# Output projection and feed-forward layer in four blocks of 512 prompt tokens and two passes over the weights, with the sample's tokens computed apart

## The chip, the cores and the metric

The kernel runs on one core of a Trainium2 chip. The core has five engines with instruction streams of their own: TensorE (PE, matmuls; its weight loads are listed as PEld), VectorE (DVE), ScalarE (ACT), GpSimd (POOL) and SyncE (SP). In this kernel nearly all transfers between DRAM and the on-chip memory SBUF are issued by SP, one behind the other: a transfer that has to wait for something holds up every transfer behind it on SP. Matmuls write into PSUM, which has eight banks of 128 x 512 fp32 numbers.

The metric is the device time of one execution in microseconds (us), the median of several runs.

## The reference

One layer with two groups of tokens: a prompt of 2048 tokens, and a sample of 8 streams with 16 tokens each (128 tokens), which have modulation vectors of their own for each stream. Model width is 1024 (8 chunks of 128), feed-forward width 2816 (22 chunks of 128). The change concerns the last lines of the layer:

```
mix = jnp.concatenate([conv_out, attn], axis=-1) @ w_out
x = x + g1 * mix
h = _rmsnorm(x, norm2_g) * (1 + sc2) + sh2
x = x + g2 * ((jax.nn.silu(h @ w_gate) * (h @ w_up)) @ w_down)
```

What lies ahead of these lines (input projection, convolution, attention) is the same code in both kernels.

## The kernel before

All numbers are fp32. For TensorE each operand is split into two fp32r parts, high and low (`parts_of`: ScalarE copies the high part, VectorE subtracts for the low one), and each product is three matmuls: high x high, low x high, high x low. Activations are transposed: 128 channels on the partitions, tokens along the columns.

**Token blocks.** The 2176 tokens (prompt and sample together) form six blocks, `HALVES`, of 368, 368 and four times 360 columns; the sample is the end of the last block. Two blocks form a pair; `PAIRS` has three.

**Output projection** (`project_out`, L1169). For each block eight accumulators take all eight PSUM banks, one for each chunk of output channels. For each of eight input chunks c, in `OUT_ORDER`, a tile of the concatenated input is loaded from DRAM (`cr<-cat_d`, a ring of four), passed through Swish for c < 4, split into `ch` and `cl`, and multiplied: 8 x 3 matmuls. Then for each of the eight banks the input x is loaded (`xo<-xT`, a ring of 20 tiles), `scaled_add` (L1141) puts x + g1 * mix into it, it is written to DRAM (`x_d<-xo`), ScalarE squares it and POOL adds the squares up (`ssum`, L1210). `root` (L1223 on) makes the reciprocal square root of the mean, with small matmuls on TensorE. The x tiles of blocks 0 and 1 stay in SBUF; pair 0 is normed from them behind block 2 (`norm`: POOL's product at L1253, ScalarE's scale and shift, VectorE's subtractions in `right_sides`).

**Feed-forward layer** (`ffn_up`, `ffn_down`). A pair's two blocks, and the two halves of the weights, make 2 x 2 block products, computed with seven products (q = 0 to 6) of sums instead of eight. `right_sides` writes the seven right sides to DRAM (`ht_d` for the up products, `gt_d` for the down products), `sums` writes the sums of weights (`sup_d`, `sdn_d`). For each pair, up has 11 column blocks f (each of two chunks u), 14 products of 12 matmuls in each; down has seven q with four products of 33 matmuls. With three pairs that is 5544 + 2772 = 8316 matmuls (L1440). Products take turns in the eight banks. The norms of pairs 1 and 2 are woven into the up products of pair 0.

**What sets the order.** Each engine's stream is in the order in which the program and its scheduler emit it. `pump` loads ahead: whenever a product has been emitted, it fills the free slots of the rings W (left sides, 6, later 10) and T (right sides, 8, later 29). Right sides pass through raw tiles of their own (`traw`, 6); weights through quarters (`rR`, 12, later 15). The pump starts only at the end of block 4 of the projection.

Of the kernel before, what the change touches and what calls it, by code (L numbers as in the profile page):

```python
# [1 line left out]

# [4 lines left out]
F32 = mybir.dt.float32  # L7
# [32 lines left out]
HALVES = [(0, 368), (368, 736), (736, 1096), (1096, 1456), (1456, 1816), (1816, 2176)]  # L40
NW = 368
PAIRS = [(HALVES[i][0], HALVES[i][1] - HALVES[i][0]) for i in (0, 2, 4)]
# [14 lines left out]
BANK8 = ("u", "cv", "tr", "u", "ss", "u", "cv", "tr")  # L57
# [61 lines left out]
class Layer:  # L119
# [30 lines left out]
    def run(self, stop=99):  # L150
# [3 lines left out]
        with ExitStack() as ctx:  # L154
# [12 lines left out]
            self.ht_d = d.tile([P, 3, 7, 4, NW], F32, name="ht_d")  # L167
            self.r_d = d.tile([len(HALVES), P, NW], F32, name="r_d")
            self.gt_d = d.tile([P, 3, 7, NF // 2, NW], F32, name="gt_d")
# [940 lines left out]
    def out_projection(self, stop):  # L1110
        self.L.close()
        with ExitStack() as c0:
            self.rings(c0)
            with ExitStack() as c1:
                self.project_out(c1)
            self.LB.close()
            self.grow(c0)
            with ExitStack() as c1:
                self.ffn_up(c1)
            with ExitStack() as c1:  # L1120
                self.ffn_down(c1)

# [4 lines left out]
    def accumulate(self, acc, terms, n, first, last):  # L1127

        for j, z in enumerate(acc):
            m = slice(j * P, (j + 1) * P)  # L1130
            for i, (hi, lo, yh, yl) in enumerate(terms):
                for k, (w, y) in enumerate(((hi, yh), (lo, yh), (hi, yl))):
                    self.nc.tensor.matmul(z[:, :n], w[:, m], y, start=(first and i == 0 and k == 0),  # L1133
                                          stop=(last and i == len(terms) - 1 and k == 2))

    def scaled_add(self, z, v, j, x, b0, b1):

        nc = self.nc
        n, npr = b1 - b0, min(b1, T) - b0
        m = self.mod[v][:, j, :]  # L1140
        nc.vector.scalar_tensor_tensor(x[:, :npr], z[:, :npr], m[:, 0:1], x[:, :npr], ALU.mult, ALU.add)  # L1141
        if npr < n:
            zv, xv = sample_view(z[:, npr:n]), sample_view(x[:, npr:n])
            nc.vector.tensor_tensor(zv, zv, per_stream(m[:, 1:9]), ALU.mult)
            nc.vector.tensor_tensor(xv, xv, zv, ALU.add)
# [6 lines left out]
    def split_rows(self, hi, lo, src, ring, tag):  # L1152

        for i in range(2):
            t = slice(512 * i, 512 * i + 512)
            raw = ring.tile([P, 512], F32, tag=tag, name="raw")
            self.queued(self.nc.sync.dma_start(raw, src[:, t]))
# [497 lines left out]
```

## Time and profile before

| | us |
|---|---|
| median of 3 runs | 2840.87 (2839.73 to 2841.87) |
| the profiled execution, its own time | 2842.93 |
| its span in the profile | 2841.2 |

The profile is of one execution. A page of it gives each engine's busy time and share of the span; other views give the chain of work that ended last (each step followed back to what released it), busy time by stretch of the span, groups of instructions by line and shape, single instructions in order of time with the idle time ahead of them, and what SP waited for. A row such as `L1440 PE MATMUL z<-rT,rW` names the line, the engine, the operation and the tiles written and read. A busy matmul row's mean is the time from its start to its end; since matmuls overlap in the pipeline, the spacing between them is shorter, and is read from starts or from a stretch in which TensorE never stops. The granted clock of TensorE is given as a share of full speed. The lines that matter stand where they are used, below.

### The profile page before, as it was taken

What the parts mean: (1) busy time and instruction counts of PE and PEld (TensorE: products, weight loads), DVE (VectorE), ACT (ScalarE), POOL (GpSimd) and SP (SyncE); (2) the same over time, 40 slices, a digit from 0 to 9 for tenths busy, and PEclk for the clock granted to TensorE, in tenths of its full rate; (3) what the DMA queues carried; (4) which work ended last, traced back from release to release, by engine and by line L of the source; (5) the groups of instructions that cost most, each with busy time, mean ns of one, the idle gap of its engine ahead of it and who ended that gap; (6) DMA issues with size and microseconds to landing.
All of it is one profiled execution on the core that took longest, in us unless ns stands there. A gap on an engine that the chain in (4) does not pass through costs nothing.

```text
span 2841.2 us, 48479 instructions
## 1 busy us (share of the span) xinstructions
PE 2729.4 (96%) x16536; PEld 2521.3 (89%) x16536; DVE 2160.8 (76%) x4235; ACT 1435.3 (51%) x2812; POOL 506.0 (18%) x685
## 2 busy tenths in 40 slices
PE   7899999989988999999998999999999999999999
PEld 6899988866666777788998999999999999999999
DVE  3698898988786788635488899777797778676765
ACT  4443323357675777754354455444454446555552
POOL 3454411243232222213202020000000000000000
PEclk9999999988899999999998999999999999999999
DMA  8763567674236656355667678776786669788883
GB/s 306 247 196 113 176 220 255 189 204 124 82 110 175 191 182 185 116 174 189 212 238 232 237 264 287 255 229 208 227 296 213 217 209 310 245 281 257 271 255 117
DMA packets 390024, 603.23 MB, mean 212 GB/s; under 512 B 46240, under 2 KB 249152, under 8 KB 387728
## 3 DMA queue, kind: packets, MB, share of 16 engines
q1 hardware_dynamic: 375312, 574.72, 62.6%
q0 software_dynamic: 14464, 25.42, 3.7%
q8 instruction: 130, 2.13, 0.3%
q14 instruction: 118, 0.97, 0.1%
HBM read 421.97 MB, written 178.07 MB: 211 GB/s over the span
## 4 chain that ended last, share of the span: by engine, by line
PE 78%; DMA 9%; DVE 6%; ACT 3%; issue 3%; POOL 2%; SPq 1%; DVEq 0%; ACTq 0%; POOLq 0%
PE z L1440 44%; PE z L510 7%; PE pv L957 5%; PE acc L1133 4%; PE pa L320 3%; PE pvv L340 3%; PE pg L320 3%; PE s L966 2%; PE s L967 2%; PE mx L927 2%; DMA vraw<-o_v 1%; DVE M L930 1%; DMA wraw<-w_in 1%; DMA k_d<-qp 1%; PE lane L1096 1%
## 5 line engine op out<-in xcount | busy, mean ns | idle before, releaser
L1440 PE MATMUL z<-rT,rW 128*128 128x360 f32 (+1 forms) x8316 | 1382.6, 328 | 5.1 <-ACT oR L1240 1.9
L1440 PEld LDWEIGHTS z<-rT,rW 128*128 128x128 f32 x8316 | 1379.4, 188 | 6.9 <-ACT oR L1240 2.3
L1149 ACT ACTIVATE rW<-rR 128x512 fp32r<-128x512 f32 x714 | 435.1, 617 | 397.9 <-PE z L1440 285.6
L1150 DVE TENSOR_TENSOR rW<-rR,rW 128x512 fp32r<-128x512 f32 x714 | 477.6, 673 | 154.7 <-ACT rW L1149 150.8
L698 DVE SCALAR_TENSOR_TENSOR cv<-cu,cpar,cv 128x384 f32<-128x384 f32 x580 | 311.6, 616 | 2.6 <-ACT cv L696 2.5
L957 PE MATMUL pv<-e,V 128*128 128x512 f32 (+3 forms) x960 | 265.0, 381 | 22.6 <-ACT e L1149 13.1
L957 PEld LDWEIGHTS pv<-e,V 128*128 128x128 f32 x960 | 168.9, 192 | 68.3 <-ACT e L1149 15.2
L930 DVE TENSOR_REDUCE M<-mx 128x1 f32<-128x512 f32 (+2 forms) x320 | 190.1, 605 | 50.5 <-PE mx L927 34.9
L971 ACT ACTIVATE ef<-s 128x512 f32<-128x512 f32 (+3 forms) x320 | 166.0, 529 | 104.8 <-PE s L967 46.7
L510 PE MATMUL z<-hqx,wqh 128*128 128x384 f32 (+1 forms) x768 | 196.6, 333 | 1.3 <-DVE logf L347 1.3
L1149 ACT ACTIVATE rT<-traw 128x360 fp32r<-128x360 f32 (+1 forms) x315 | 149.9, 501 | 88.8 <-DMA traw<-gt_d 52.5
L1150 POOL TENSOR_TENSOR e<-ef,e 128x512 fp32r<-128x512 f32 (+3 forms) x106 | 127.0, 1198 | 364.4 <-ACT e L1149 182.1
L1150 DVE TENSOR_TENSOR rT<-traw,rT 128x360 fp32r<-128x360 f32 (+1 forms) x315 | 158.4, 533 | 41.3 <-ACT rT L1149 41.0
L1150 DVE TENSOR_TENSOR e<-ef,e 128x512 fp32r<-128x512 f32 (+3 forms) x214 | 147.3, 698 | 40.8 <-ACT e L1149 38.1
L1149 ACT ACTIVATE e<-ef 128x512 fp32r<-128x512 f32 (+3 forms) x320 | 174.2, 565 | 4.4
L510 PEld LDWEIGHTS z<-hqx,wqh 128*128 128x128 f32 x768 | 135.7, 188 | 19.2 <-issue 15.5
L927 PE MATMUL mx<-K,Q 96*128 96x512 f32 (+2 forms) x320 | 133.6, 426 | 15.3 <-DVE M L930 13.2
L1133 PE MATMUL acc<-ch,woh 128*128 128x360 f32 (+1 forms) x384 | 128.4, 336 | 9.9 <-ACT ch L1149 5.0
L1368 DVE TENSOR_TENSOR rR<-rR 128x512 f32<-128x512 f32 (+1 forms) x136 | 90.5, 683 | 54.6 <-DMA rR<-w_down 50.0
L966 PE MATMUL s<-Q,K 128*128 128x512 f32 (+3 forms) x320 | 126.7, 397 | 3.2 <-ACT ef L971 3.0
L1133 PE MATMUL acc<-ch,wol 128*128 128x360 f32 (+1 forms) x384 | 128.1, 334 | 0.0
L510 PE MATMUL z<-hqx,wql 128*128 128x384 f32 (+1 forms) x384 | 126.4, 329 | 0.0
(306 smaller groups left out, 3955.5 us busy)
## 6 DMA issues: line engine op xcount, KB each, us to landing
rR<-sup_d SPq DMA_DIRECT2D x176, 256.0 KB
rR<-w_gate SPq DMA_DIRECT2D x132, 256.0 KB
traw<-gt_d SPq DMA_DIRECT2D x154, 180.0 KB
rR<-w_down SPq DMA_DIRECT2D x104, 256.0 KB
rR<-sdn_d SPq DMA_DIRECT2D x96, 256.0 KB
rR<-w_up SPq DMA_DIRECT2D x88, 256.0 KB
sup_d<-rR SPq DMA_DIRECT2D x88, 256.0 KB
wa<-w_ada SPq DMA_DIRECT2D x16, 1024.0 KB
```

The source lines that it names most:

```text
L320: nc.tensor.matmul(pz[:, :n], w[:, m], x[:, :n], start=(c == 0 and k == 0), stop=(c == CB - 1 and k == 2))
L510: nc.tensor.matmul(z[:, :n], w[:, m], x[:, :n], start=(c == 0 and k == 0), stop=(c == CB - 1 and k == 2))
L698: self.pin(nc.vector.scalar_tensor_tensor(dst, src, w, acc[i], ALU.mult, ALU.add))
L927: nc.tensor.matmul(mx[:, :w], Q2[0:AUX, h, j * P:(j + 1) * P], K2[kb][0:AUX, h, :w], start=True, stop=not diag)
L930: nc.vector.tensor_reduce(M[:, i, kb:kb + 1], mx[:, :w], AX.X, ALU.max)
L957: nc.tensor.matmul(z[h][:, off:], V[kt // 4][:, v, kt % 4, h:h + 2, :].rearrange("p b c -> p (b c)"), e[:, x, off:], start=(kt == 0 and i ...
L966: nc.tensor.matmul(s[:, off:], K1[kb][:, h, sl], Q1[:, h, off:], start=True, stop=False)
L971: nc.scalar.activation(ef[:, off:], s[:, off:], AF.Exp)
L1133: self.nc.tensor.matmul(z[:, :n], w[:, m], y, start=(first and i == 0 and k == 0), stop=(last and i == len(terms) - 1 and k == 2))
L1149: self.nc.scalar.activation(hi, raw, AF.Copy)
L1150: engine.tensor_tensor(lo, raw, f32(hi), ALU.subtract)
L1440: nc.tensor.matmul(z, W[:, x, m], t[:, y, :w], start=(k == 0 and i == 0), stop=(k == n - 1 and i == 2))
```

## The change

The blocks are now four of 512 prompt columns, the widest that a bank holds, in two pairs, so that the weights are gone through twice. The 128 sample tokens leave the blocks. Their activations become left sides (`lhsT`) of plain products with 512 columns of weights, in three places: between blocks 1 and 2 of the projection (`sample`, 48 matmuls), in the up products of pair 1 (`sample_up`, 264 matmuls, weights `w_gu` loaded and split for it) and in the down products of pair 0 from its product 6 on (`sample_down`, 132 matmuls, weights `w_dn`, left sides `gS` loaded from `gs_d`). Their results come out transposed and are turned back by 8 + 22 + 8 transposes on TensorE.

Counts: products of the feed-forward layer 4 x 1386 = 5544 matmuls in place of 8316, and 396 for the sample; projection 768 + 48 in place of 1152. All have 512 columns.

To make room in SBUF the buffers change:

| | before | after |
|---|---|---|
| x tiles of the projection | 20 | 5 |
| raw tiles | cat 4, w_out 3, right sides 6, weights in their quarters | one ring of 5 for cat and w_out and first right sides; 4 in up pass 0; then one ring of 5 for left and right sides, sample's weights and `gS` |
| T slots | 8, later 29 | 8, 24 with block 3 of the projection (in the room of w_out), 28 |
| W slots | 6, later 10 | 6, 7 from up pass 1 |
| banks that products rotate in | 8 | 5 (the sample uses the others) |
| x of pair 0 for its norm | kept in SBUF | loaded again (`nx<-x_d`) |

Pair 0's norm is spread over block 2 (two steps behind each c), drained behind it, and the pump starts there, ahead of block 3 in the program. The core of the diff:

```diff
-HALVES = [(0, 368), (368, 736), (736, 1096), (1096, 1456), (1456, 1816), (1816, 2176)]
-PAIRS = [(HALVES[i][0], HALVES[i][1] - HALVES[i][0]) for i in (0, 2, 4)]
-BANK8 = ("u", "cv", "tr", "u", "ss", "u", "cv", "tr")
+NW = 512
+HALVES = [(b, b + NW) for b in range(0, T, NW)]
+PAIRS = [(HALVES[i], HALVES[i + 1]) for i in (0, 2)]
+BANK5 = ("u", "cv", "u", "cv", "u")
+SAMPLE_AT = (0, 2, 4, 5, 7, 9, 11, 12)
...
+    def loaded(self, t, src, func=None, queued=False):
+        pool, tag, n = self.raw
+        raw = pool.tile([P, 512], F32, tag=tag, name="raw", bufs=n)[:, :src.shape[-1]]
+        load = self.nc.sync.dma_start(raw, src)
...
+        self.parts_of(hi, lo, raw, self.nc.vector)
...
     def project_out(self, ctx):
+        self.raw = cp, "cr", 5
...
+        def block(b0, b1, work):
+            acc = self.accumulators()
+            tail = []
+            for i, c in enumerate(OUT_ORDER):
+                tail.append((*weights(c), cat(c, b0, b1)))
+                if b1 < T or i < CB - 2:
+                    self.accumulate(acc, tail, i == 0, i == CB - 1)
+                    tail = []
+                for _ in range(2):
+                    next(work, None)
...
-                x = sp.tile([P, NW], F32, tag="x", name="xo", bufs=20)
+                x = sp.tile([P, NW], F32, tag="x", name="xo", bufs=5)
...
+        for b0, b1 in HALVES[:2]:
+            sums.append(block(b0, b1, none))
+            nload += 1
+        sample()
+        norm = self.norm(0, sp, [self.root(s, NW, sp) for s in sums])
+        for i, (b0, b1) in enumerate(HALVES[2:]):
+            s = block(b0, b1, norm)
+            nc.sync.dma_start(self.r_d[2 + i], s)
+            if i == 0:
+                drain(norm)
+                self.normed = 1
+            else:
+                self.free["T"].extend([None] * 16)
+            self.pump()
...
+    def sample_part(self, z, x, first, last):
+        W = self.used("W")
+        for i, (y, w) in enumerate(((0, 0), (1, 0), (0, 1))):
+            self.nc.tensor.matmul(z, x[:, y], W[:, w], start=(first and i == 0), stop=(last and i == 2))
+        self.pump()
...
     def ffn_down(self, ctx):
+        sample = self.sample_down(sp)
+        for p in range(2):
+            E = [{} for _ in range(4)]
+            for i in range(28):
+                q, j = i // 4, i % 4
+                self.product(NF // 2, self.rights_of(0, NF // 2), lambda z: evac(E[j], p, j, q, z), j == 3)
+                if p == 0:
+                    for _ in self.down_sample(i):
+                        next(sample)
...
+    def sample_down(self, sp):
+        z = [self.bank("tr", "zs") for _ in range(2)]
+        for k in range(NF):
+            x = sp.tile([P, 2, P], F32R, tag="gS", name="gS", bufs=6)
+            self.loaded(x, self.gs_d[:, k])
+            for h in range(2):
+                self.sample_part(z[h], x, k == 0, k == NF - 1)
+                yield
```

The order of each engine's instructions up to the end of attention is the same. Three places behind it, as the instruction streams have them (line, operation, tiles written and read, shape, number of instructions in a row; DMA rows are issues).

SP around the change from block 0 to block 1 of the projection, before: `cr<-cat_d` loads an input chunk, `xo<-xT` loads x, `x_d<-xo` writes x1.

```order
L1184 DMA cr<-cat_d 128x368
L1199 DMA xo<-xT 128x368 x8
L1184 DMA cr<-cat_d 128x368 x6
L1203 DMA x_d<-xo 128x368 x8
L1184 DMA cr<-cat_d 128x368 x2
```

And in the changed kernel, where `raw<-cat_d` is the load of an input chunk:

```order
L1164 DMA raw<-cat_d 128x512
L1219 DMA xo<-xT 128x512 x5
L1223 DMA x_d<-xo 128x512 x3
L1219 DMA xo<-xT 128x512
L1223 DMA x_d<-xo 128x512 x2
L1219 DMA xo<-xT 128x512 x2
L1164 DMA raw<-cat_d 128x512 x2
L1223 DMA x_d<-xo 128x512
L1164 DMA raw<-cat_d 128x512 x3
```

Before, all eight x loads and six of the next block's chunk loads stand ahead of the first x1 write; now five x loads do, the other three stand between the writes, and block 1's chunk loads stand behind them.

ScalarE at the same place, in the changed kernel: squares of block 0 (`ssum`, `sqo`) and high parts of block 1's chunks (`cat<-raw`).

```order
L1225 ACTIVATE ssum<-xo 128x512
L1228 ACTIVATE sqo<-xo 128x512 x6
L1157 ACTIVATE cat<-raw 128x512
L1228 ACTIVATE sqo<-xo 128x512
L1157 ACTIVATE cat<-raw 128x512 x3
```

Seven of the eight squares stand ahead of the first chunk of the next block.

SP between block 2 and block 3, before: the chunk loads (`cr<-cat_d`) of block 3 and the norm's writes of right sides (`ht_d<-xo`).

```order
L1219 DMA r_d<-ssum 128x360
L1184 DMA cr<-cat_d 128x360
L1295 DMA ht_d<-xo 128x368
L1184 DMA cr<-cat_d 128x360
L1295 DMA ht_d<-xo 128x368 x2
L1295 DMA ht_d<-ot_14360 128x368
```

And in the changed kernel, ahead of the first two chunk loads of block 3: `r_d<-ssum` writes block 2's sum of squares, `nx<-x_d` loads x1 for the norm, `ht_d<-nx` writes right sides, `raw<-ht_d` loads T.

```order
L1266 DMA r_d<-ssum 128x512
L1302 DMA nx<-x_d 128x512 x2
L1219 DMA xo<-xT 128x512
L1306 DMA ht_d<-nx 128x512
L1219 DMA xo<-xT 128x512
L1306 DMA ht_d<-nx 128x512
L1164 DMA raw<-ht_d 128x512 x2
L1347 DMA ht_d<-nx 128x512 x2
L1164 DMA raw<-ht_d 128x512
L1347 DMA ht_d<-nx 128x512
L1164 DMA raw<-ht_d 128x512 x2
L1164 DMA raw<-cat_d 128x512 x2
```

Before, chunk loads stood among the writes; now all of them stand behind the end of the norm and five T loads.

POOL over the last blocks of the projection in the changed kernel: the adds of squares (`ssum`) of blocks 0 and 1, then the norm's products (`nx`) around the adds of block 2.

```order
L1229 TENSOR_TENSOR ssum<-ssum,sqo 128x512 x14
L1303 TENSOR_TENSOR nx<-nx,oR 128x512 x12
L1229 TENSOR_TENSOR ssum<-ssum,sqo 128x512 x7
L1303 TENSOR_TENSOR nx<-nx,oR 128x512 x4
L1229 TENSOR_TENSOR ssum<-ssum,sqo 128x512 x7
```

Before, eight of the sixteen products stood ahead of block 2's adds and eight behind them; now twelve and four.

ScalarE in the down products of pair 0, at a change of q, in the changed kernel: high parts of W, of T and of the sample's left sides (`gS`), each from the one raw ring.

```order
L1157 ACTIVATE rW<-raw 128x512 x4
L1157 ACTIVATE rW<-raw 128x384
L1157 ACTIVATE rT<-raw 128x512 x2
L1157 ACTIVATE rW<-raw 128x512
L1157 ACTIVATE rT<-raw 128x512 x2
L1157 ACTIVATE rW<-raw 128x512
L1157 ACTIVATE rT<-raw 128x512 x7
L1157 ACTIVATE gS<-raw 128x128
L1157 ACTIVATE rW<-raw 128x384
L1157 ACTIVATE rW<-raw 128x512 x4
```

Eleven T and two W stand ahead of a `gS`, in the order in which they pass through the ring of five.

TensorE there (`z` is a product, `zs` the sample's part, six matmuls behind each product from product 6 on):

```order
L1504 MATMUL z<-rT,rW 128x512 x66
L1518 MATMUL zs<-rW,gS 128x512 x6
L1504 MATMUL z<-rT,rW 128x512 x24
L1518 MATMUL zs<-rW,gS 128x512 x2
```

Before, TensorE had only products in the down stretch; now each of pair 0's products from product 6 on (counted from 0) is followed, up to one product later, by a sample part.

More of the change, by code (lines that the diff above doesn't have):

```diff
@@ L1150, in parts_of @@
         engine.tensor_tensor(lo, raw, f32(hi), ALU.subtract)
[L1152 to L1157, printed above, removed]
-            self.parts_of(hi[:, t], lo[:, t], raw, self.nc.vector)
+    def loaded(self, t, src, func=None, queued=False):
+        pool, tag, n = self.raw
+        raw = pool.tile([P, 512], F32, tag=tag, name="raw", bufs=n)[:, :src.shape[-1]]
+        load = self.nc.sync.dma_start(raw, src)
+        if queued:
+            self.queued(load)
+        elif self.last_load is not None:
+            self.after(load, self.last_load)
+        if func:
+            func(raw)
+        hi, lo = t if type(t) is tuple else (t[:, 0], t[:, 1])
+        self.parts_of(hi, lo, raw, self.nc.vector)
+        return t
     def queued(self, ins):
@@ L1211, in project_out @@
[L1211 to L1221 removed]
+                    nc.scalar.activation(sq, x, AF.Square)
@@ new lines, in block, with sample @@
+                    nc.gpsimd.tensor_tensor(ssum, ssum, sq, ALU.add)
+            return ssum
+        def sample():
+            z = [self.bank("u", "zs") for _ in range(2)]
+            for i, c in enumerate(OUT_ORDER):
+                t = cat(c, T, TT)
+                for h in range(2):
+                    for k, (x, w) in enumerate(((0, 0), (1, 0), (0, 1))):
+                        nc.tensor.matmul(z[h], t[:, x], W[c][w][:, 512 * h:512 * h + 512], start=(i == 0 and k == 0),
+                                         stop=(i == CB - 1 and k == 2))
+            ssum = sp.tile([P, 2, P], F32, tag="sss", name="sss")
+            for h in range(2):
+                s, x, sq = (sp.tile([P, NW], F32, tag=k, name=k + "s", bufs=n) for k, n in (("x", 5), ("x", 5), ("sq", 2)))
+                nc.scalar.copy(s, z[h])
+                zt = self.bank("cv", "zst")
+                self.turned(zt, s, 4)
+                at = slice(4 * h, 4 * h + 4)
+                nc.sync.dma_start(x.rearrange("p (c t) -> p c t", c=4), a["xT"][:, at, T:])
+                self.of_sample(s, 2, h, ALU.mult, zt)
+                nc.vector.tensor_tensor(x, x, s, ALU.add)
+                nc.sync.dma_start(self.x1_d[:, at, T:], x.rearrange("p (c t) -> p c t", c=4))
+                nc.scalar.activation(sq, x, AF.Square)
+                nc.vector.tensor_reduce(ssum[:, h, :], sq.rearrange("p (c t) -> p t c", c=4), AX.X, ALU.add)
+            nc.vector.tensor_tensor(ssum[:, 0, :], ssum[:, 0, :], ssum[:, 1, :], ALU.add)
+            nc.sync.dma_start(self.r_d[4, :, :P], ssum[:, 0, :])
@@ L1327, in slot @@
-        return pool.tile(shape, dt, tag=tag, name="r" + kind)
+        place = self.free[kind].popleft()
+        t = place[0].tile([P, 2, 512], F32R, tag=place[1], name="r" + kind) if place else self.wide("rT", shape=(P, 2, 512))
+        self.made[kind].append((t, place))
+        return t
     def pump(self):
-        for k, made, gen in (("W", self.W, self.next_w), ("T", self.T, self.next_t)):
-            while len(made) < self.used[k] + len(self.ring[k]) and next(gen, None):
-                pass
+        for kind, gen in self.makers.items():
+            while self.free[kind] and next(gen, None):
+                pass
```

425 lines of the change are left out of this document (234 added, 191 removed).

## The prediction

> **What bounds the kernel now.** I read the busy shares on the page first, then the chain that ended last, and then cut the span where the work changes, which shows where that chain has slack.
>
> ```profile
> PE 2729.4 (96%) x16536; PEld 2521.3 (89%) x16536; DVE 2160.8 (76%) x4235; ACT 1435.3 (51%) x2812; POOL 506.0 (18%) x685
> PE 78%; DMA 9%; DVE 6%; ACT 3%; issue 3%; POOL 2%; SPq 1%; DVEq 0%; ACTq 0%; POOLq 0%
> ```
>
> TensorE is busy for 96% of the span and is 78% of the chain. The rest of the chain is not spread evenly. The next view is busy time by stretch (length; PE, PEld, DVE, ACT, POOL with instruction counts; clock; DMA share; GB/s). The stretches: everything up to the end of attention, the output projection, the start of the feed-forward layer, and the rest of it; behind these are the second half alone (the down products) and the tail.
>
> ```profile
> 0.00:1220.80 1220.80, 1137.84 (x6970) 935.32 (x6970) 963.80 (x1912) 660.57 (x1308) 403.34 (x595) 0.96 0.58 180
> 1220.80:1432.90 212.10, 200.94 (x1186) 198.64 (x1186) 95.62 (x187) 85.91 (x163) 56.24 (x55) 0.97 0.59 191
> 1432.90:1623.20 190.30, 177.08 (x1039) 174.11 (x1037) 167.24 (x354) 90.53 (x176) 26.41 (x24) 0.96 0.73 246
> 1623.20:2836.40 1213.20, 1213.17 (x7343) 1213.17 (x7344) 932.97 (x1784) 598.30 (x1166) 20.00 (x12) 1.00 0.76 244
> 2372.00:2836.40 464.40, 464.40 (x2808) 464.40 (x2807) 322.59 (x625) 242.71 (x485) 0.00 (x0) 1.00 0.78 250
> 2836.40:2841.20 4.80, 0.33 (x2) 0.03 (x1) 1.13 (x2) 0.00 (x0) 0.00 (x0) 1.00 0.11 38
> ```
>
> From 1623 to 2836 us TensorE never stops and its clock is 1.00: there only the number and length of matmuls count, and nothing that waits can be won. All slack lies between 1220 and 1623. Up to 1220.80 the order of instructions is the same in both kernels, so I leave that stretch alone.
>
> **The change, part by part.** Each part is priced against the profiled run (2842.93 us, span 2841.2), which stands 2.1 us above the median 2840.87.
>
> *1. Fewer, wider matmuls.* The down stretch gives one matmul at the mean width (368+360+360)/3 = 362.7: 464.40/2808 = 0.1654 us. For 512 columns attention has four in a row:
>
> ```profile
> 690.17 1.07 PE L957 MATMUL pv<-e,V 128*128 128x512 f32 x4
> 691.08 0.39 PE L966 MATMUL s<-Q,K 128*128 128x512 f32 x1
> L957 PE MATMUL pv<-e,V x960: 218/391/796, 627.7 to 1221.1; 128*128 128x512 f32 x136, 128*128 128x384 f32 x20, 128*128 128x256 f32 x20, 128*128 128x128 f32 x16
> ```
>
> From the first of the four to the next matmul 0.91 us pass: 0.2275 us each. Feed-forward: 8316 x 0.1654 = 1375.5 before; now 5544 + 396 for the sample = 5940 x 0.2275 = 1351.4. Projection: 1152 x 0.1654 = 190.5; now 768 + 48 = 816 x 0.2275 = 185.6. Together **-29 us**. The bounds: time in proportion to columns (0.2335 each) gives +11; the shortest recorded duration, 0.218, taken as the spacing, gives -93. I take the row of four, since it is a spacing at full rate.
>
> A rule to weigh here: the Trainium skill, page "TensorE: Matmul & The Clock Gate", section "Wait — 56ns, not 53.3ns?", has a warm gap of N/2.4 ns plus about 2.5 ns. By it the columns nearly alone would count: 362.7 columns would take about 154 ns and 512 about 216 ns, an estimate by that page, so that 2712 fewer matmuls would save only some 7 us, the sample's added columns would cost 10, and part 1 would be about +4; this speaks against the change. The rows disagree on the size of the fixed part: 165.4 and 227.5 ns are each 12 to 14 ns above that page's time for the columns.
>
> *2. Transposes of the sample.* 8 + 22 + 8 = 38 new ones on TensorE. The nearest row is a lane transpose of the same size:
>
> ```profile
> L1078 PE MATMUL lane<-ident,S 128*128 128x128 f32 x64 | 9.8, 276 | 0.0
> ```
>
> 9.8/64 = 0.153 each, so **+6**, between 0 (they fall into a wait) and +10 (0.276 each).
>
> *3. The start of the feed-forward layer.* Before, 1432.9 to 1623.2 holds 8316 - 7343 = 973 products' matmuls, which need 973 x 0.1654 = 160.9; 29.4 us are lost. They go to VectorE and to the roots (square roots of the norms) woven in:
>
> ```profile
> 1460.00:1480.00 20.00, 20.00 (x126) 19.99 (x125) 20.00 (x40) 9.65 (x18) 0.00 (x0) 1.00 0.62 213
> 1500.00:1520.00 20.00, 17.09 (x72) 16.38 (x73) 14.16 (x30) 9.49 (x19) 6.43 (x6) 0.65 0.56 180
> 1495.11 1.13 PE L1238 MATMUL pr<-odg,sp 90*128 90x90 f32 x8 [3.21 <-DVE odg L1237]
> 1500.97 2.02 PE L1238 MATMUL pr<-odg,sp 90*128 90x90 f32 x8 [2.83 <-DVE odg L1237]
> L1150 DVE TENSOR_TENSOR rW<-rR,rW 128x512 fp32r<-128x512 f32 x630 | 431.8, 689 | 111.8 <-ACT rW L1149 109.1 <-DMA gt_d<-et 0.2 <-DMA rR<-w_gate 0.2
> ```
>
> VectorE is full (20.00 of 20.00), TensorE waits 3.21 and 2.83 us for a root, and then 20 us run at a clock of 0.65. Two column blocks f now take 168 matmuls x 0.2275 = 38.2 us instead of 168 x 0.1654 = 27.8, while VectorE's some 44 operations (14 splits, 8 weight sums, 16 of evacuation, 4 right sides, a norm's share) are at most 44 x 0.689 = 30.3 us: about 80% full. With three roots instead of four and one wide pair to norm, I keep 12 of the 29 us: **-17**, between 0 (the roots still stop TensorE) and -27.
>
> *4. The changes of block 0 to 1 and 1 to sample.* The ring of x goes from 20 tiles to 5, so loads 6 to 8 wait until an x1 write has landed; all eight cat loads of the next block stand behind them on SP, and on ScalarE seven squares stand ahead of the first split. SP's waits of before (waiter, releaser: us, times, longest) and pieces of the chain (start, us):
>
> ```profile
> SPq L1184 <- DVE cl L1150: 25.3, 9, 10.6
> SPq L1199 <- DMA x_d<-xo: 2.6, 7, 1.0
> 1262.29 3.98 DMA cr<-cat_d
> 1272.20 3.81 DMA xo<-xT
> 1331.46 3.94 DMA x_d<-xo
> L1141 DVE SCALAR_TENSOR_TENSOR xo<-acc,mod,xo 128x360 f32<-128x360 f32 x24 | 12.6, 585 | 3.4 <-DMA xo<-xT 3.3
> L1149 ACT ACTIVATE rW<-rR 128x512 fp32r<-128x512 f32 x630 | 392.0, 629 | 340.2 <-PE z L1440 236.5 <-issue 31.4 <-DVE rR L1368 22.0
> ```
>
> The first row shows that SP does stand still behind one wait. Let T0 be the block's last matmul. Accumulator 1 is done 18 matmuls earlier, T0-4.1; its add (0.585 x 512/360 = 0.83) ends at T0-3.3, its write is issued some 0.3 later and lands 3.94 later, T0+1.0; the seventh x load lands 3.81 later, T0+4.8; add, square (0.63) and split (0.63) end at about T0+7, when TensorE may start. Two changes: **+14**. The bounds are 0 (loads land early enough; before, these changes cost TensorE almost nothing) and +18 with a slow clock behind each.
>
> *5. The change of block 2 to 3.* Behind block 2 SP has, in its order: the write of the sum of squares r_d, two norm loads, the writes of the last right sides, T loads of them, and only then the cats of block 3. POOL adds seven sums before the last four norm products. The rows:
>
> ```profile
> L1210 POOL TENSOR_TENSOR ssum<-ssum,sqo 128x360 f32<-128x360 f32 x28 | 27.9, 997 | 87.1 <-ACT sqo L1209 85.7
> L1150 POOL TENSOR_TENSOR e<-ef,e 128x512 fp32r<-128x512 f32 x74 | 100.2, 1355 | 302.6 <-ACT e L1149 140.6 <-PE mx L929 59.7 <-PE s L967 25.4
> 1548.83 2.36 DMA nx<-x_d
> 1358.08 2.26 DMA ht_d<-ot
> 1365.61 3.75 DMA cr<-cat_d
> ```
>
> The eighth x arrives by T0+5.7 as in part 4; with add, square and a POOL add (997 ns at 360 columns; 1355 for another form at 512) the sum is there at T0+8.5. Then: norm loads issued and landed, 3.2; two POOL products, 2.7; ScalarE, 0.7; three subtractions and their issues, 2.5; the cat's landing, 3.75; its split, 0.63: 13.5 us more, TensorE starts at T0+22. With some 1.5 of slow clock **+24**. It reaches from 15 (the eighth x already there) to 32 (T loads wait for the ht_d writes too, 2.26 each). Before, x stayed in SBUF, chunk loads stood among the writes on SP, and TensorE hardly waited.
>
> *6. Down products of pair 0.* From product 6 on, each product (33 + 6 matmuls, 8.9 us) needs 3 W, 2 sample W, 1 gS and on average 2.75 T through one raw ring of 5. A turn of a slot is landing (3.18 to 4.07), split high (0.63) and low (0.69), some 0.5 for issue: 5.0 to 5.9, or 1.0 to 1.18 us a raw.
>
> ```profile
> 1315.75 3.18 DMA traw<-ht_d
> 1320.80 4.07 DMA traw<-ht_d
> 2400.00:2429.00 29.00, 29.00 (x175) 29.00 (x174) 22.48 (x43) 16.76 (x33) 0.00 (x0) 1.00 0.94 314
> ```
>
> At the six transitions of q, 11 T and 2 W stand ahead of a gS: it is ready 0.7 + 5.0 + 13 turns = 19 to 22 us after the product's start, while TensorE, after two products and a sample part, comes to it at 16.4. About 4 us each: **+24**, between 0 (loads run ahead in the slack between transitions) and 50 (DMA at 0.94 already, before the sample's loads are added).
>
> *7. The rest.* Small gaps inside the old projection (about 6 us, a row under the rivals) go; the sample's evacuations and the passage from up pass 0 to 1, with a burst of loads through the ring, should bring as much: 0.
>
> Sum: -29 + 6 - 17 + 14 + 24 + 24 = **+22**, or 2865 for the profiled run and **2863** against the median.
>
> One more page bears on the waits: the Trainium skill, "TensorE: Matmul & The Clock Gate", section "What's actually happening", has the clock halved by an idle window of about 3.4 us. The trace agrees in kind (0.65 after waits of 3.21 and 2.83). By that rule each wait of parts 4 and 5 would pay for a cold start as well, which the slow-clock allowances of those parts already hold.
>
> **Rivals.**
> - *Waits hidden, faster.* The place is the ring of x (parts 4, 5) and the gS loads (part 6). If x loads land before they are needed and T loads run ahead in the slack between transitions, parts 4 and 6 fall to some 4 together and part 5 to 15: 2841 - 40 + 19 = 2820. It decides at 40 us of waits in all: below, not slower. For it: before, block changes cost TensorE little (in the row below 5.5 us, most of it ended by VectorE's adds), and the down stretch never waited in spite of a DMA share of 0.94. Against: rings of 20 and separate rings stood there.
>
> ```profile
> L1133 PE MATMUL acc<-ch,woh 128*128 128x360 f32 x256 | 84.6, 333 | 5.5 <-DVE xo L1141 3.8 <-ACT oR L1240 1.1 <-ACT ch L1149 0.6
> ```
>
> - *Waits at the break-even.* Parts 4 to 6 at about 40: no change, 2841.
> - *The raw ring bounds all of pair 0's down products.* At 1.18 us x 8.75 = 10.3 us a product instead of 8.9, 22 products lose 31 instead of 24, and pass 1 of up and the T bursts of pair 1 lose some 15: about 2885. For it: SP's waits on splits, 10.6 us long. Against: W and T run ahead.
> - *Matmul time in proportion to columns, no fixed part saved.* Part 1 is +11 instead of -29: 2903. The row of four speaks against it. The rule of the Trainium skill's page weighed in part 1 goes this way, too.
> - *Wide matmuls at the shortest record, 0.218.* Part 1 is -93 instead of -29: 2799. The row of four speaks against this as well.
>
> **How the numbers follow.** The forecast's own case (2850 to 2876) has 0.47; waits hidden 0.24; break-even 0.11; ring bound 0.11; proportional 0.03; 0.218 us 0.04. Measurement tells about 0.2%, 5.7 us, from no change. Faster: 0.24 + 0.04 = 0.28; same 0.11; slower 0.47 + 0.11 + 0.03 = 0.61. The range runs from 2815, which holds most of the hidden case, to 2900, which holds the ring case with part 5 at its end; what is out is the 0.218 and proportional cases and the tails of the others, under 0.2.
>
> **What would show it.** Part 1: an undisturbed stretch of z at 0.2275 us each. Part 3: VectorE at about 80% in up pass 0. Parts 4 and 5: TensorE idle of 7, 7 and over 15 us before the first cat split of blocks 1, sample and 3, released by ScalarE. Part 6: six waits before zs, ended by the gS split. The forecast is wrong if TensorE's idle time behind 1231 us is under 40 us, or if 512 columns take other than 0.22 to 0.235.

## The result, and the profile after

The changed kernel takes 2925.99 us (median of 4 runs, 2919.03 to 2930.42) against 2841.37 us of the kernel before on the same chip (4 runs): ratio 1.0295, 95% interval 1.027 to 1.032. It is about 85 us slower. The direction was forecast, the size was not: 2863 was forecast, and the range ended at 2900.

The page of the changed kernel, busy shares and the chain that ended last:

```profile
span 2928.6 us, 41249 instructions
PE 2751.8 (94%) x13846; PEld 2233.0 (76%) x13846; DVE 2066.7 (71%) x3686; ACT 1361.6 (46%) x2512; POOL 483.2 (16%) x655
PE 72%; DMA 13%; DVE 7%; ACT 3%; issue 2%; POOL 1%; SPq 1%; ACTq 0%; DVEq 0%; POOLq 0%
```

There are 2690 fewer matmul records (13846 against 16536), and yet TensorE is busy for 22 us longer (2751.8 against 2729.4). Its share of the chain has gone from 78% to 72%, and that of transfers from 9% to 13%. So two things happened: the matmuls together did not get cheaper, and there is more waiting.

Busy time by stretch (columns as in the same view of before): projection from the end of attention to the first product; up to the last root; up to the first sample part of the down products; while sample parts run in the down products; the rest.

```profile
1219.60:1486.90 267.30, 207.81 (x858) 165.94 (x858) 104.74 (x172) 94.04 (x154) 55.46 (x42) 0.87 0.58 195
1486.90:1634.40 147.50, 146.33 (x658) 119.01 (x657) 126.29 (x218) 64.41 (x107) 26.26 (x19) 1.00 0.70 238
1634.40:2467.70 833.30, 833.27 (x3606) 674.66 (x3605) 615.70 (x972) 353.24 (x607) 0.00 (x0) 1.00 0.64 212
2467.70:2730.50 262.80, 233.10 (x925) 181.07 (x926) 148.88 (x247) 117.43 (x214) 0.00 (x0) 0.92 0.70 216
2730.50:2923.40 192.90, 192.90 (x833) 156.14 (x832) 105.12 (x163) 72.72 (x125) 0.00 (x0) 1.00 0.61 190
```

The third and the last row are pure TensorE, as most of before was. The first has a clock of 0.87 and 59 us without TensorE, the fourth 0.92 and 30 us. TensorE in order of time, with the idle time ahead of an instruction and what ended it:

```profile
1230.39 0.80 PE L1136 MATMUL acc<-cat,woh 128*128 128x512 f32 x1 [10.75 <-ACT cat L1157]
1285.08 0.80 PE L1136 MATMUL acc<-cat,woh 128*128 128x512 f32 x1 [6.77 <-ACT cat L1157]
1339.78 1.41 PE L1280 MATMUL pr<-sp,ssum 128*128 128x2 f32 x6 [6.82 <-DVE xo L1141]
1439.54 0.80 PE L1136 MATMUL acc<-cat,woh 128*128 128x512 f32 x1 [32.43 <-ACT cat L1157]
1634.61 290.04 PE L1504 MATMUL z<-rT,rW 128*128 128x512 f32 x1250
2471.29 1.28 PE L1518 MATMUL zs<-rW,gS 128*128 128x512 f32 x3 [3.62 <-ACT gS L1157]
2495.40 1.22 PE L1518 MATMUL zs<-rW,gS 128*128 128x512 f32 x2 [5.48 <-ACT gS L1157]
2730.57 193.22 PE L1504 MATMUL z<-rT,rW 128*128 128x512 f32 x831
```

The waits of the prediction are all there: ahead of block 1 and of the sample's part 6.8 us each, ahead of block 3 32.4 us, and ahead of sample parts in the down products. One of them ends otherwise than forecast: ahead of the sample's part TensorE waits for VectorE's add of x, with a small matmul of a root, and not for a chunk's split on ScalarE. The last row gives the price of a wide matmul: 193.22/831 = 0.2325 us, and the row of 1250 gives 290.04/1250 = 0.2320; 0.2275 was forecast.

**The sum, by measured terms.** 6756 matmuls x 0.2323 = 1569.4 us against 9468 x 0.1654 = 1566.0: +3. The projection lost 21 us before (211.6 from the end of attention to the first product, less 1152 x 0.1654) and loses 78 now (267.3 - 816 x 0.2323): +57. The start of the feed-forward layer lost 29 us and loses 6 now (147.5 - 610 x 0.2323): -23. The down products with sample parts, 918 matmuls of 0.2323 in 262.8 us, lose 49.6 us, and lost nothing before: +50. Of these 49.6, 29.7 are time without TensorE (262.8 less 233.1); the rest, some 20 us, is that its matmuls there took 233.1 us instead of 213.3, at a granted clock of 0.92. Together +87; the span is 87.4 us longer.

**Block 2 to 3.** SP and POOL in order of time there; TensorE's last matmul of block 2 ends at 1407.1.

```profile
1418.85 3.08 POOL L1229 TENSOR_TENSOR ssum<-ssum,sqo 128x512 f32<-128x512 f32 x2 [2.12 <-ACT sqo L1228]
...
1421.95 0.32 SPq L1266 DMA_DIRECT2D r_d<-ssum  x1
1422.32 0.90 SPq L1302 DMA_DIRECT2D nx<-x_d  x2
...
1428.41 0.80 SPq L1164 DMA_DIRECT2D raw<-ht_d  x2
...
1433.41 0.99 SPq L1164 DMA_DIRECT2D raw<-cat_d  x2
```

The write of the sum goes out 14.8 us behind the block's end, where 8.5 was forecast; the first chunk load of block 3 goes out 11.5 us later, and TensorE starts 6.1 us behind that. What made the sum late stands on VectorE:

```profile
1408.68 0.90 DVE L1346 TENSOR_TENSOR nx<-nx 128x512 f32<-128x512 f32 x1 [3.60 <-DMA x_d<-xo]
...
1414.18 3.10 DVE L1346 TENSOR_TENSOR nx<-nx 128x512 f32<-128x512 f32 x2 [1.29 <-DMA ht_d<-nx]
1417.23 1.61 DVE L1141 SCALAR_TENSOR_TENSOR xo<-acc,mod,xo 128x512 f32<-128x512 f32 x2
```

The norm's right sides are made in place, so a subtraction waits until the write of what it overwrites has landed (1.29 us), and it and the next one (3.10 us together) hold up the last two adds of x behind them, on which the sum of squares hangs. An earlier subtraction stands behind 3.60 us of waiting.

**Down products of pair 0.** The chain that ended last, pieces in order of time, in the stretch where T loads run:

```profile
2387.61 3.48 DMA raw<-gt_d
...
2391.18 0.64 ACT rT L1157
...
2392.45 0.68 DVE eU L1585
2393.14 0.09 DVE rW L1158
...
2393.65 0.24 DVE rT L1158
...
2394.26 0.70 DVE rT L1158
2394.97 3.65 DMA raw<-gt_d
...
2402.29 3.68 DMA raw<-gt_d
```

From one load of a slot to its next pass 7.36 and 7.32 us, where 5.0 to 5.9 were forecast: landing (3.48) and splitting are as assumed, but the low split stands behind other work on VectorE for some 2 us (ready at 2391.82, started at 2394.26).

### The profile page after: what moved, and what is told of

The parts are those of the page before. It is cut to its first block, busy times and chain, and to the rows that moved or that the text cites. A ratio compares the mean times of both kernels' runs of the same rounds, so it can differ in the third digit from the quotient of the medians.

```text
span 2928.6 us, 41249 instructions
## 1 busy us (share of the span) xinstructions
PE 2751.8 (94%) x13846; PEld 2233.0 (76%) x13846; DVE 2066.7 (71%) x3686; ACT 1361.6 (46%) x2512; POOL 483.2 (16%) x655
## 4 chain that ended last, share of the span: by engine, by line
PE 72%; DMA 13%; DVE 7%; ACT 3%; issue 2%; POOL 1%; SPq 1%; ACTq 0%; DVEq 0%; POOLq 0%
PE z L1504 36%; PE z L515 6%; PE acc L1136 5%; PE pv L962 5%; DMA raw<-gt_d 3%; PE pvv L345 3%; PE pa L325 3%; PE zs L1518 3%; PE pg L325 2%; PE s L971 2%; PE mx L932 2%; PE s L972 2%; DMA vraw<-o_v 2%; DMA ht_d<-nx 1%; DVE M L935 1%
## 5 line engine op out<-in xcount | busy, mean ns | idle before, releaser
L1504 PE MATMUL z<-rT,rW 128*128 128x512 f32 x5544 | 1320.8, 397 | 8.7 <-ACT rW L1157 7.6
L1504 PEld LDWEIGHTS z<-rT,rW 128*128 128x128 f32 x5544 | 1045.6, 189 | 258.6 <-ACT rW L1157 11.3
L1157 ACT ACTIVATE rW<-raw 128x512 fp32r<-128x512 f32 (+1 forms) x454 | 274.2, 616 | 349.1 <-PE z L1504 204.2
L1158 DVE TENSOR_TENSOR rW<-raw,rW 128x512 fp32r<-128x512 f32 (+1 forms) x454 | 300.1, 673 | 165.8 <-ACT rW L1157 163.0
L1158 DVE TENSOR_TENSOR rT<-raw,rT 128x512 fp32r<-128x512 f32 x210 | 143.0, 698 | 111.0 <-ACT rT L1157 110.4
L1136 PE MATMUL acc<-cat,woh 128*128 128x512 f32 x512 | 167.9, 407 | 50.7 <-ACT cat L1157 49.9
L1157 ACT ACTIVATE rT<-raw 128x512 fp32r<-128x512 f32 x210 | 130.8, 629 | 135.9 <-DMA raw<-gt_d 93.5
L1157 ACT ACTIVATE rW<-rR 128x512 fp32r<-128x512 f32 x154 | 97.0, 631 | 145.5 <-PE z L1504 125.6
L1136 PEld LDWEIGHTS acc<-cat,woh 128*128 128x128 f32 x512 | 99.6, 195 | 76.3 <-ACT cat L1157 51.0
L1158 DVE TENSOR_TENSOR rW<-rR,rW 128x512 fp32r<-128x512 f32 x154 | 109.5, 712 | 48.7 <-ACT rW L1157 47.4
```

What stands on the lines that cost most here:

```text
L1136: self.nc.tensor.matmul(z, w[:, m], y[:, x], start=(first and i == 0 and k == 0), stop=(last and i == len(terms) - 1 and k == 2))
L1157: self.nc.scalar.activation(hi, raw, AF.Copy)
L1158: engine.tensor_tensor(lo, raw, f32(hi), ALU.subtract)
L1504: nc.tensor.matmul(z, W[:, x, m], T[k][:, y], start=(k == 0 and i == 0), stop=(k == n - 1 and i == 2))
```

## The experiments

All durations by stretch are of one profiled execution; the ratio is of all runs to those of the kernel before on the same chip. Between executions the stretch ahead of the change ends between 1212 and 1227 us, so that single executions are compared from there on.

| kernel | median us | ratio (95%) | end of attention to first product | first to last product |
|---|---|---|---|---|
| before | 2841.37 | 1 | 211.6 | 1403.3 |
| changed | 2925.99 | 1.0295 (1.027 to 1.032) | 267.3 | 1436.5 |
| changed, addresses (a1_pad) | 2916.89 | 1.0247 (1.0219 to 1.0274) | 261.9 | 1424.3 |
| changed, T late (a4_late) | 2909.24 | 1.0236 (1.0206 to 1.0266) | 249.3 | 1439.1 |
| changed, x chain (a5_xq) | 2915.83 | 1.0251 (1.0228 to 1.0273) | 251.3 | 1435.5 |
| changed, ring of 11 (a2_ring) | 2887.65 | 1.0167 (1.0151 to 1.0182) | 265.8 | 1396.4 |
| changed, gS early (a3_gs) | 2908.01 | 1.0241 (1.0224 to 1.0258) | 265.4 | 1412.4 |
| changed, ring and gS (a23) | 2883.30 | 1.0163 (1.0137 to 1.0188) | 267.9 | 1390.0 |
| changed, all repairs (a6_all7) | 2828.98 | 0.9958 (0.9943 to 0.9973) | 213.9 | 1389.1 |
| the same, T behind 7th chunk (a6_all6) | 2824.57 | 0.9947 (0.993 to 0.9963) | 215.3 | 1381.1 |
| the same without addresses (a7_nopad) | 2839.54 | 0.9998 (0.9987 to 1.0009) | 214.7 | 1394.5 |
| before, addresses (b1_pad) | 2837.37 | 0.9975 (0.9961 to 0.9989) | 211.6 | 1399.1 |
| before, addresses, again (b1_again) | 2832.58 | 0.9971 (0.996 to 0.9982) | 209.8 | 1400.3 |

### The price of a wide matmul: start addresses

Why 0.2323 and not 0.2275? First, the four matmuls of L957 that gave the price are the fastest row of their kind. The trace of before has 57 rows of four to eight matmuls of L957 with 512 columns at a granted clock of 1.00. From the first of a row to the next other matmul they take 0.2265 (that row, by its unrounded starts) to 0.264 us each, and half of the rows are over 0.24. One of them, with 1.89/8 = 0.236 us each:

```profile
905.87 2.05 PE L957 MATMUL pv<-e,V 128*128 128x512 f32 x8
907.76 0.39 PE L966 MATMUL s<-Q,K 128*128 128x512 f32 x1
```

Then, what sets the spacing within the feed-forward layer? The traces hold no addresses; I took the address of each product's right side from the built program and put it beside the starts in the trace. Of the last 831 products' matmuls, the 264 whose right side starts at a multiple of 64 bytes are 229.0 ns apart on average, the 566 that start 32 bytes off 233.9 ns. The edit moves all the latter by 32 bytes:

```diff
+            pad = ctx.enter_context(self.pool(name="pad", bufs=1, side="right")).tile([P, 8], F32, name="pad")
+            self.nc.gpsimd.memset(pad, 0.0)
             self.big = self.LB.enter_context(self.pool(name="big", bufs=16, side="right"))
```

> The changed kernel with 32 bytes of unused memory at the right end of SBUF, so that every right side T and every part of w_out starts at a multiple of 64 bytes; nothing else. In the trace of the changed kernel the products whose T starts at a multiple of 64 are 227 ns apart, those 32 bytes off 233 ns. Theory (the start address sets the spacing): all products stand 227 ns apart, the stretch of the last 831 products takes 831 x 0.227 = 188.6 us instead of 193.0, and the part of the span behind attention gets shorter by about 0.8 x 6756 x 6 ns = 30 us; the stretches ahead, whose right-hand tiles move too, may gain as well. Rival (the pool, or what VectorE, ScalarE and the transfers do beside it, sets the spacing): it stays at 232 ns, no change within 0.2%.

TensorE in the changed kernel with moved addresses, to be read against the 193.22 above:

```profile
2708.06 190.84 PE L1506 MATMUL z<-rT,rW 128*128 128x512 f32 x831
```

The products whose right side was moved came from 233.9 to 229.5 ns, those that had been at a multiple of 64 stayed (229.0 and 229.4). So the start address counts at 512 columns, but it explains about half of what lay between forecast and trace: 0.2297 us on average now, not 0.227. The rest still goes by the right side: in both traces the spacing has nearly the same pattern in the four products of a q, which share their right sides, and with moved addresses it reaches from 227 to 235 ns (means over the three matmuls of a right side); why is open. The gain is 0.48 points of the ratio, 14 us (the intervals of the two ratios just overlap), and the profiled executions differ by 12 us in the feed-forward layer; 30 were expected.

The same for the kernel before, where it takes paddings in three places (the pool above, one at the left end, one behind `spread`):

```diff
             self.keep = ctx.enter_context(self.pool(name="keep", bufs=1))
+            pad = self.keep.tile([P, 8], F32, name="padl")
...
         self.spread = ones, mean, ident = [cp.tile([P, k], F32, name=f"sp{i}") for i, k in enumerate((P, 2, P))]
+        pad = cp.tile([P, 8], F32, name="pads")
```

> The kernel before with unused memory of 32 bytes in three places, so that the left sides W, the right sides T and w_out start at multiples of 64 bytes; nothing else. There every W starts 32 bytes off, and products of 360 columns are 165 ns apart. Theory (the start address, of the left side too): they come to about 161 ns, the shortest tenth of the records, and 9468 matmuls gain some 4 ns each, 35 to 40 us behind attention. Rival (only the right side's address counts, or neither): 165 ns as before, no change.

The theory fell at this width. Behind 1620 us products of 360 columns are 163.9 ns apart on average where they were 164.6, and those of 368 are at 167.7 where they were 167.2. The kernel is 0.25% faster; of the feed-forward layer's time only 4 us went. At 360 columns the address counts for almost nothing, at 512 for 4 to 5 ns.

Then the fixed part itself, by width in one kernel:

```diff
+        w = (512, 448, 384, 368, 360, 256, 128)[self.nbank % 14 // 2]
...
-                nc.tensor.matmul(z, W[:, x, m], T[k][:, y], start=(k == 0 and i == 0), stop=(k == n - 1 and i == 2))
+                v = 512 if k == 0 and i == 0 else w
+                nc.tensor.matmul(z[:, :v], W[:, x, m], T[k][:, y, :v], start=(k == 0 and i == 0), stop=(k == n - 1 and i == 2))
```

> The changed kernel in which eleven of each four-step product's twelve matmuls (32 of 33 in the down products) use only the first 512, 448, 384, 368, 360, 256 or 128 columns of the right side, the width changing with the place of the product among seven pairs; the other columns are left out of the sums. It measures the spacing of back-to-back matmuls by width with the same operands. Theory (time goes with the columns, with almost no fixed part): a line through the widths has a fixed part under 5 ns, some 0.45 ns a column; 256 columns about 117 ns. Rival (the prediction's fixed part of about 13 ns at 0.417 ns a column): 256 columns about 120, 360 about 163, and 128 about 67 ns against 58 by the theory.

From one execution, the median spacing of neighbouring matmuls of one width, some 500 pairs each: 231 ns at 512 columns, 203 at 448, 175 at 384, 169 at 368, 166 at 360, 119 at 256, and 112 at 128. A line through the widths from 256 up has 0.436 ns a column and a fixed part of 8 ns: neither under 5 nor 13. From 256 to 128 columns the spacing hardly falls, which neither expected. With these numbers 512 columns cost 1.392 times as much as 360 (231/166) and have 1.422 times the columns: 2% are saved by width in this kernel. Between the kernels of before and after it is less: 0.2323/512 against 0.1654/362.7 saves 0.5% a column, and the columns that the sample adds (6756 x 512 against 9468 x 362.7, 0.7% more) take that back. With moved addresses (0.2297) it is 1.6%. The Trainium skill, page "TensorE: Matmul & The Clock Gate", section "Wait — 56ns, not 53.3ns?", has 215.7 ns for 512 columns once warm; here the products of 512 columns came to 229 ns on average at best, at a granted clock of 1.00. By what came of part 1 (+3 us) its rule (+4) was much nearer than my -29; by the fixed part measured here, 8 ns, its 2.5 was as far off as my 13.

### Blocks 0 to 1 and 1 to the sample: the chain of loads

```diff
-                if nload < 2:
+                if nload < 2 and j < 5:
                     self.queued(load)
```

> The changed kernel in which the last three x loads of blocks 0 and 1 are no longer chained on SP ahead of the next block's chunk loads; the ring of x stays at 5. Theory (SP's order, not the ring, makes the waits of 6.8 us at the changes 0 to 1 and 1 to sample): both fall under 3 us, some 8 to 14 us gained. Rival (the ring: the accumulators of the last three banks are freed late whatever SP does): TensorE waits for the banks instead, by VectorE's adds, and 0 to 5 us are gained.

With the ring of x left at 5, the wait ahead of block 1 is gone and the one ahead of the sample's part has become

```profile
1333.64 0.50 PE L1239 MATMUL zs<-woh,cat 128*128 128x512 f32 x1 [1.26 <-DVE cat L1158]
```

in the kernel with loads 6 to 8 unchained. The projection is 16 us shorter, although the wait ahead of block 3 grew to 37.2; the runs give 0.44 points, 12 us, and the intervals of the two ratios just overlap. The theory holds by the two waits: SP's order made them. The small ring alone did not.

### Block 2 to 3: the norm's end and the T loads

```diff
+            def late():
+                drain(norm)
+                self.normed = 1
+                self.pump()
...
-            s = block(b0, b1, norm)
+            s = block(b0, b1, norm, late if i else None)
             nc.sync.dma_start(self.r_d[2 + i], s)
-            if i == 0:
-                drain(norm)
-                self.normed = 1
-            else:
+            if i:
```

> The changed kernel with the end of pair 0's norm and the first eight T loads moved from behind block 2 to the middle of block 3 (behind its fourth chunk); nothing left out. Theory (block 3's chunk loads stand on SP behind the norm's end and the T loads): TensorE's idle time of 32.4 us ahead of block 3 falls under 8 us, and the kernel is 25 to 30 us faster. Rival (the wait is only moved, since the T loads are then late for the first products): the idle time comes back within block 3 or at the start of the feed-forward layer, under 8 us gained.

In this kernel, whose `block` calls `late` behind the fourth chunk, four chunks of block 3 are multiplied with one wait of 0.94 us, and then comes

```profile
1452.39 0.80 PE L1136 MATMUL acc<-cat,woh 128*128 128x512 f32 x1 [14.02 <-ACT cat L1157]
```

Of 32.4 us 14.0 are left; 17 us were gained, not 25 to 30, and neither expectation was met. On ScalarE five high parts of T now stand ahead of the fifth chunk, and T hangs on the end of the norm. The kernel with all repairs, further down, calls it behind the eighth chunk, and there 2.77 us are left ahead of block 3, ended by VectorE's add of x and no longer by a chunk. So what stands ahead of the chunks is the cause, the norm's end and the T loads, on SP first and then on ScalarE; the two were not tried apart.

### The down products: ring and order

```diff
+        more = ctx.enter_context(self.pool(name="raw2", bufs=1))
+        self.raw = [self.raw] * 5 + [(more, "raw2", 6)] * 6
...
-        pool, tag, n = self.raw
+        pool, tag, n = self.raw[self.nraw % len(self.raw)] if type(self.raw) is list else self.raw
+        self.nraw += 1
```

> The changed kernel with 6 more raw tiles in the ring of the down products (11 in place of 5), nothing else. In the changed kernel the stretch from the first wait of a sample part to the last (2467.7 to 2730.6 us, 918 products' matmuls of 0.2323) lost 49.6 us. Theory (the ring of 5 bounds it: a slot's turn is landing, splits and issue): with 11 the loss falls under 15 us, 35 us gained. Rival 1 (the gS load stands too late, behind the T burst): a wider ring lets T pass faster too, but a wait of 2 to 5 us at each of the six changes of q stays, under 20 gained. Rival 2 (the transfers' bandwidth): no gain.

The feed-forward layer is 40 us shorter, the runs give 1.28 points, 36 us; one wait of 2.96 us (for a W) and one of 1.39 us are left behind 2430 us. The room was there: the six tiles, 12 KB of each partition, fit in beside the others.

```diff
-            x = sp.tile([P, 2, P], F32R, tag="gS", name="gS", bufs=6)
-            self.loaded(x, self.gs_d[:, k])
+            while ahead and len(xs) < 5:
+                xs.append(sp.tile([P, 2, P], F32R, tag="gS", name="gS", bufs=6))
+                self.loaded(xs[-1], self.gs_d[:, ahead.popleft()])
+            x = xs.popleft()
```

> The changed kernel with the sample's left sides gS loaded up to four steps ahead in the program, ring of 5 kept. Theory (ring of 5): the wait only moves from gS to the W behind it, under 12 us gained. Rival 1 (position of gS): the six waits ahead of zs go, 25 to 35 us gained.

Between the two: 24 us by the stretch, 15 us by the runs. TensorE, in the kernel with gS early:

```profile
2497.84 1.52 PE L1504 MATMUL z<-rT,rW 128*128 128x512 f32 x2 [5.40 <-ACT rW L1157]
```

The wait that had been 5.48 for gS is now 5.40 for a W behind the same T burst; the first and the later waits got shorter. So the place of gS is a part of the cause, but the ring is what each load waits for.

> The changed kernel with both: 11 raw tiles in the down products and gS loaded up to four steps ahead. Theory (ring): as with the wider ring alone, within 5 us. Rival 1 (position): at least 10 us more than the wider ring alone.

Both together: 46.5 of the 49.6 us by the stretch, 1.32 points by the runs, and their interval covers that of the wider ring alone. The ring was enough.

### All repairs

The edits above together, `late` behind the eighth chunk, and each block's chunk loaded ahead of its w_out:

```diff
-                tail.append((*weights(c), cat(c, b0, b1)))
+                y = cat(c, b0, b1)
+                tail.append((*weights(c), y))
```

> The changed kernel with all repairs: start addresses at multiples of 64, x loads 6 to 8 out of the chain, block 3's T loads behind its last chunk, each block's chunk ahead of its w_out, 11 raw tiles and early gS in the down products. If the terms are independent: 2926 less about 9 (addresses), 13 (x chain), 25 (block 2 to 3), 4 (start), 40 (down) = 2835 us, level with the kernel before or up to 0.5% faster. If they share a cause (each wait only moves to the next engine), under half of the sum is gained: over 2880.

2828.98 us, 0.42% faster than the kernel before: the gains add up, and the rival (under half of the sum) is out. The largest waits that are left behind block 2, in this kernel's TensorE rows:

```profile
1386.33 0.66 PE L1138 MATMUL acc<-cat,woh 128*128 128x512 f32 x1 [2.77 <-DVE xo L1143]
1454.16 1.22 PE L1512 MATMUL z<-rT,rW 128*128 128x512 f32 x2 [7.60 <-ACT eU L1587]
```

> All repairs as before, with the T loads behind the seventh chunk of block 3 instead of the eighth. If the wait of 7.6 us at the start of the feed-forward layer came from T loads that start too late, it falls under 4 us and the kernel is 2 to 6 us faster than with the eighth (2829): about 2825. If the wait comes from the evacuation of block 3 (x loads behind them on SP), no gain or a loss of up to 5.

With T behind the seventh chunk the wait of 7.60 became two of 3.40 and 3.07, and the median 2824.57; the intervals of the two overlap. By stretch, in this fastest kernel (projection, start of the feed-forward layer, the rest):

```profile
1215.40:1430.70 215.30, 197.49 (x858) 158.28 (x857) 94.18 (x160) 87.85 (x143) 49.48 (x37) 0.97 0.67 224
1430.70:1582.30 151.60, 146.46 (x657) 120.09 (x658) 133.11 (x230) 69.86 (x118) 37.29 (x23) 0.99 0.75 257
1582.30:2811.80 1229.50, 1227.77 (x5362) 1004.04 (x5362) 862.46 (x1383) 537.33 (x945) 0.00 (x0) 1.00 0.66 219
```

The wait of 10.8 us at the very start of the projection is still there (10.82): to put the chunk ahead of w_out was no repair. Before, 4.41 us stood there. What differs is again the order on SP, where attention's last write waits for VectorE (`cat_d<-pvs`, columns that block 0 does not read). Before, the first four chunk loads stood ahead of it:

```profile
1219.32 1.85 SPq L1184 DMA_DIRECT2D cr<-cat_d  x4
...
1226.30 0.33 SPq L996 DMA_DIRECT2D cat_d<-pvs  x1
```

In the changed kernel they stand behind it and the sample's four writes:

```profile
1224.59 0.33 SPq L1001 DMA_DIRECT2D cat_d<-pvs  x1
1224.96 1.88 SPq L826 DMA_DIRECT2D cat_d<-catS  x4
1226.94 1.88 SPq L1164 DMA_DIRECT2D raw<-cat_d  x4
```

SP stood 9.3 us ahead of that write, in the fastest kernel too. So the order of the streams is not quite the same up to the end of attention. No run moved these loads back; that it would take the 6 us away is not shown.

> The same, without the 32 bytes that move the start addresses. If those were worth what they were worth alone (about 9 us, of which some 7 lie ahead of the changed part): 8 to 12 us slower than with them, about 2835. If the repairs of order and ring do not depend on them, still not slower than the kernel before by over 0.2%.

Without the moved addresses the repaired kernel is level with the one before (0.9998). The addresses are worth 0.51 points here, 14 us, 13 of them in the feed-forward layer; in the kernel before 0.25 to 0.29 points.

> The kernel before with the three paddings once more, beside the two kernels above on the same chip, to see whether the changed kernel with all repairs beats it too. By the first comparison it is 0.25% faster than before (0.11 to 0.39%) and the repaired one 0.42% (0.27 to 0.57%): the repaired one 3 to 8 us faster than this one.

By medians the repaired kernel is 8 us faster than the kernel before with moved addresses (2824.57 and 2832.58), but the intervals of their ratios (0.993 to 0.9963, and 0.996 to 0.9982) just overlap. With the addresses alike in both, with paddings or without (0.9998), a gain of the wide blocks themselves is not shown.

## Why the prediction was right in direction and wrong in size

1. **Fewer, wider matmuls: wrong, and the step that decided.** Forecast -29, measured +3. "I take the row of four, since it is a spacing at full rate" failed: the row was the fastest of its kind. In the same trace half of the rows like it are over 0.24 us a matmul (57 rows, above). The projection of q and k, too, ran 384 columns at 173 ns (median), which in proportion is 231 at 512. The rival with no fixed part saved (+11) had 0.03 and was much nearer. About half of the gap between 0.2275 and 0.2323 goes with the start address (shown); what the other half is stays open.
2. **Transposes: right.** They come in twos, fours and eights. By starts the 38 take some 4 us (1.58 for the first eight, 0.14 for each of eleven twos, 0.83 for the last eight); +6 was forecast, with 0 as the lower bound.
3. **Start of the feed-forward layer: right in cause, larger.** Forecast -17, measured -23: VectorE is busy 126.29 of 147.50 us (86%) and all that is lost there, roots included, is 6 us.
4. **Blocks 0 to 1 and 1 to the sample: right in the waits, short by the slow clock.** Forecast 7 us each, measured 6.77 and 6.82, and the released chain took them away; the second was ended by VectorE's add, not by ScalarE. But each is followed by a slow clock, which the +14 left to its upper bound of 18: 0.85 and 0.84 in the 20 us behind these two waits, some 3 us each.
5. **Block 2 to 3: right in cause, too small.** Forecast 22 of idle time and some 1.5 of slow clock, measured 32.4 and about 3. The term that was most too small is the time to the sum of squares: 14.8 us, not 8.5, since VectorE's in-place subtractions wait for writes ahead of the adds. From there to TensorE's start it took 17.6 us, not 13.5.
6. **Down products: right in cause, and a term left out.** Forecast 24, measured 49.6. The waits alone came to 29.7, not far from the forecast; the slot's turn was 7.3 us instead of 5.0 to 5.9, or 1.46 us a raw. The other 20 us are slow clock behind these waits (0.92 over the stretch), for which part 6, unlike part 5, had no term. The upper bound of 50 had the sum, but for another reason (transfers).
7. **The rest: wrong.** Forecast 0. The first wait of the projection grew from 4.41 to 10.75 us, with SP's order as shown above, and behind each long wait of the projection the clock is low for a while: 0.84 to 0.86 over the 20 us behind the waits of 6.8 to 32.4 us and 1.00 later in the blocks, 0.87 on average over the stretch.

So of the 65 us that lie between the forecast and the profiled execution (+22 and +87), 32 are the price of a wide matmul, 26 the down products (20 of them slow clock), and 18 the projection (10 of idle time ahead of block 3, 6 at its start, the rest slow clock); the start of the feed-forward layer and the transposes give some 10 back. The range held none of these errors added together: it took the cases one by one, while the errors lie in parts that add up, as the repairs did.

## What to carry to other kernels

Read the price of a wider instruction from all rows of its kind, and from several widths in the same kind of loop, not from one short row; here the width itself saved 0.5 to 2% a column. Where a wait is priced, price the slow clock behind it too. When rings are cut to make room for wider tiles, price a slot's whole turn, with the work that stands ahead of the split on its engine, against what TensorE eats, and look at what else stands in the same queue: the whole loss of 85 us went with six more tiles in a part where there was room, and with loads put into another order (0.9998, without moved addresses). A load that many steps need (the next block's chunk, a small left side) should not stand behind a burst that only needs to be there later.

## What the runs showed of the hardware that was not expected

- Matmuls of 128 x 128 by 512 fp32r columns are 4 to 5 ns slower where the right side starts 32 bytes off a multiple of 64 (233.9 and 229.5 ns for the same tiles moved by 32 bytes). At 360 and 368 columns, where the left sides were moved too, nothing of that size was seen (164.6 and 163.9, 167.2 and 167.7).
- Spacing by width: 0.436 ns a column and 8 ns, but 112 ns at 128 columns, hardly less than the 119 at 256.
- Paddings of 32 bytes in three places made the kernel before 0.25 to 0.29% faster, and at most 4 us of that lie in the feed-forward layer, at which it was aimed. Where the rest lies is not settled: attention ends at 1212 to 1221 us in the five profiled executions with moved addresses, and at 1215 to 1227 in the eight without.
